# Low parts of the mixers' weights: a negated high part plus an accumulating DMA in place of a subtraction

## The chip, the cores and the metric

One Trainium2 chip, one core. The metric is the device time of one execution in microseconds (us), the median of several runs. The engines are called PE or TensorE (matrix products), DVE or VectorE, ACT or ScalarE, POOL or GpSimd, and SP or SyncE, which here issues the loads.

## The reference

A decoder trunk of two layers on 512 tokens of width 1024 in float32. Cut to what matters:

```python
def hybrid_layer(x, mem, pos, layer_idx, ...):
    proj = rms_norm(x, norm_mix) @ w_in              # one combined input projection
    if layer_idx % 2 == 0:
        mix, qm = dsa_mixer(proj, pos)               # index scores, top 128 keys of a query, softmax attention
    else:
        mix, qm = dilated_mixer(proj, pos)           # three groups of dilated windows, merged
    mo = memory_attention(qm, mem, norm_mem, w_mem_kv)   # 4 heads on 256 memory tokens
    x = x + concat([mix, mo]) @ w_out                # one combined output projection
    return x + swiglu_ffn(rms_norm(x, norm_ffn), w_gate_up, w_down)
# two layers, then a final rms_norm
```

## The kernel before

Activations lie transposed in SBUF, 128 rows of the width by 512 tokens. Every product of float32 numbers is made of three products in a format with a shorter mantissa, fp32r: a weight is split into a high part `wh` (the weight rounded) and a low part `wl` (what is left), an activation into `xh` and `xl`, and TensorE adds wh·xh, wh·xl and wl·xh (lines 200 to 202, 213 to 215, 225 to 227 and 405 to 407). For a tile of 128 columns of weights and 512 tokens these are 24 matrix products.

Weights come from DRAM by `load` (line 176 issues it on SP) into `wf`, 128x2048 float32 with two buffers; each half of 128x1024 is then split by `wsplit` into one of three buffers `wh` and one of three `wl`. `_split2` does it in two instructions: a cast, on ScalarE (line 48) or VectorE (line 50), and a subtraction `wl = wf - wh`, on VectorE or POOL (line 51). Who does which is set by arguments. There are 55 such splits of 128x1024 in the mixers:

- `chunks` gives the column tiles of an input projection or of the memory's keys, two to a load: in layer 0 tiles 2 to 14 of `in0` and 2 of `mk0`, in layer 1 2 of `mk1` and 14 of `in1`. The first tile of a load is subtracted on POOL, the second on VectorE; tiles 6 to 14 of `in0` both on POOL.
- `token_weights` gives weights with the tokens as output rows, for values (`vw0`; `mv0`, `mv1` of the memory; `v1` three times). The first half is subtracted on VectorE, the second on POOL; for `v1` the first half's cast is on VectorE too.
- `out_proj` gives the output projections (`out0a`, `out0b`, `out0c`, `out1a`, `out1b`, 12 splits): the cast on VectorE, the subtraction on POOL.

The first two weights of layer 0 and all of the feed-forward parts are split elsewhere by the same `wsplit`.

The order of TensorE's instructions is written out by hand. Those of the other engines are placed by a scheduler when the program is built; it goes by costs of its own and not by a run. An engine works through its list in that order and waits at the head of it. In layer 0 the memory's squares and their sum (`mem`, `ssq`, lines 282 and 294) are on POOL, with tables of line 373 and products of lines 338 and 339; VectorE has the top-k (lines 702 and 703: 48 maximum searches, each followed by a replacement), evictions of the memory's values (`vm`, line 387) and row maxima (`nm`, line 557). Products land in PSUM, in 2 banks of `acc`, 3 of `S`, 2 of `T` and 1 of `O`.

## Time and profile before

| | |
|---|---|
| three runs | 1286.81, 1294.6, 1292.8 us |
| median | 1292.8 us |
| profiled execution | span 1288.0 us from first to last instruction (its time with what lies around the span is not listed) |
| granted clock of TensorE | 0.974 of full speed, mean |
| TensorE busy | 1212.7 us, 94% |
| VectorE, ScalarE, POOL busy | 626.6, 532.1, 402.6 us |
| read from DRAM | 106 MB |

The table's busy times are sums over the whole span; the stages differ. Layer 0's mixer runs to about 313 us, its feed-forward part to 672, layer 1's mixer to 907 and its feed-forward part and the final norm to the end. In the rows further down, a trace line has its start in us from the span's start, its length in us, the engine, the line of the kernel, the operation, output and inputs with their shapes, and in brackets the idle time of the engine just before it and what ended that.

### The profile page before, as it was taken

What the parts mean: (1) busy time and instruction counts of PE and PEld (TensorE: products, weight loads), DVE (VectorE), ACT (ScalarE), POOL (GpSimd) and SP (SyncE); (2) the same over time, 40 slices, a digit from 0 to 9 for tenths busy, and PEclk for the clock granted to TensorE, in tenths of its full rate; (3) what the DMA queues carried; (4) which work ended last, traced back from release to release, by engine and by line L of the source; (5) the groups of instructions that cost most, each with busy time, mean ns of one, the idle gap of its engine ahead of it and who ended that gap; (6) DMA issues with size and microseconds to landing.
All of it is one profiled execution on the core that took longest, in us unless ns stands there. A gap on an engine that the chain in (4) does not pass through costs nothing.

```text
span 1288.0 us, 15199 instructions
## 1 busy us (share of the span) xinstructions
PE 1212.7 (94%) x5868; PEld 996.6 (77%) x5868; DVE 626.6 (49%) x1154; ACT 532.1 (41%) x941; POOL 402.6 (31%) x250
## 2 busy tenths in 40 slices
PE   6689888998999999999998999999999999999997
PEld 4567667776888888888886779897788888888887
DVE  7789978758433333332214554548733333331212
ACT  6554667744322233322223666644433222322222
POOL 4637475436222222212232213232522222221222
PEclk9789999999999999999998999989999999999999
DMA  5402222111222222222233110101122222222221
GB/s 179 132 32 70 80 84 96 53 63 66 95 91 90 91 93 98 98 90 102 90 110 115 66 66 34 66 34 66 66 98 98 98 98 98 98 83 97 91 90 66
DMA packets 30214, 110.52 MB, mean 86 GB/s; under 512 B 2494, under 2 KB 11582, under 8 KB 21694
## 3 DMA queue, kind: packets, MB, share of 16 engines
q1 hardware_dynamic: 29598, 109.02, 24.0%
q8 instruction: 46, 0.75, 0.2%
q10 hardware_dynamic: 544, 0.52, 0.1%
q14 instruction: 26, 0.21, 0.0%
HBM read 106.00 MB, written 3.54 MB: 85 GB/s over the span
## 4 chain that ended last, share of the span: by engine, by line
PE 74%; DVE 4%; ACT 2%; DMA 1%; issue 1%; SPq 0%; DVEq 0%; ACTq 0%
PE psS L227 5%; PE psS L226 5%; PE psS L225 4%; PE psT L227 3%; PE psT L226 3%; PE psT L225 3%; PE psacc L227 3%; PE psacc L226 3%; PE psacc L225 3%; PE psS L200 3%; PE psS L202 3%; PE psS L201 3%; PE psacc L200 3%; PE psacc L201 3%; PE psacc L202 3%; PE psacc L213 2%
## 5 line engine op out<-in xcount | busy, mean ns | idle before, releaser
L51 POOL TENSOR_TENSOR wl<-wf,wh 128x1024 fp32r<-128x1024 f32 x98 | 239.4, 2444 | 660.3 <-ACT wh L48 614.7
L48 ACT CAST wh<-wf 128x1024 fp32r<-128x1024 f32 (+1 forms) x178 | 183.5, 1032 | 515.9 <-issue 165.2
L51 DVE TENSOR_TENSOR wl<-wf,wh 128x1024 fp32r<-128x1024 f32 (+1 forms) x95 | 115.6, 1217 | 86.7 <-ACT wh L48 86.7
L225 PE MATMUL psS<-xh,wh 128*128 128x512 f32 x296 | 117.5, 397 | 7.4 <-ACT wh L48 7.4
L226 PE MATMUL psS<-xl,wh 128*128 128x512 f32 x296 | 117.2, 396 | 2.9 <-DVE xl L310 2.9
L227 PE MATMUL psS<-xh,wl 128*128 128x512 f32 x296 | 118.0, 399 | 1.1 <-DVE wl L51 0.7
L225 PE MATMUL psT<-xh,wh 128*128 128x512 f32 x200 | 80.0, 400 | 0.0
L227 PE MATMUL psT<-xh,wl 128*128 128x512 f32 x200 | 79.9, 400 | 0.0
L226 PE MATMUL psT<-xl,wh 128*128 128x512 f32 x200 | 79.7, 398 | 0.0
L227 PE MATMUL psacc<-xh,wl 128*128 128x512 f32 x192 | 76.0, 396 | 0.0
L226 PE MATMUL psacc<-xl,wh 128*128 128x512 f32 x192 | 75.7, 394 | 0.0
L225 PE MATMUL psacc<-xh,wh 128*128 128x512 f32 x192 | 75.3, 392 | 0.0
L225 PEld LDWEIGHTS psS<-xh,wh 128*128 128x128 f32 x296 | 56.2, 190 | 20.6 <-ACT wh L48 7.9
L226 PEld LDWEIGHTS psS<-xl,wh 128*128 128x128 f32 x296 | 56.3, 190 | 16.6 <-DVE xl L310 3.3
L227 PEld LDWEIGHTS psS<-xh,wl 128*128 128x128 f32 x296 | 56.3, 190 | 14.2 <-DVE wl L51 2.2
L294 POOL TENSOR_TENSOR ssq<-ssq,t 128x512 f32<-128x512 f32 (+1 forms) x34 | 49.1, 1444 | 57.7 <-ACT t L284 56.6
L659 DVE TENSOR_TENSOR raw<-psacc,R 128x512 f32<-128x512 f32 x22 | 15.2, 691 | 100.8 <-PE psacc L227 100.8
L213 PE MATMUL psacc<-xh,wh 128*128 128x512 f32 x144 | 62.7, 435 | 0.4 <-DVE vm L387 0.4
L215 PE MATMUL psacc<-xh,wl 128*128 128x512 f32 x144 | 58.4, 406 | 0.0
L214 PE MATMUL psacc<-xl,wh 128*128 128x512 f32 x144 | 58.4, 406 | 0.0
L339 POOL TENSOR_TENSOR raw<-raw,table 128x512 f32<-128x512 f32 x21 | 27.1, 1291 | 71.8 <-ACT raw L336 52.1
L634 DVE TENSOR_TENSOR xT<-xT,psacc 128x512 f32<-128x512 f32 x44 | 29.9, 684 | 34.7 <-PE psacc L202 34.3
(355 smaller groups left out, 2947.3 us busy)
## 6 DMA issues: line engine op xcount, KB each, us to landing
wf<-in_gu SPq DMA_DIRECT2D x44, 1024.0 KB
wf<-in_dn SPq DMA_DIRECT2D x16, 1024.0 KB
wf<-in_in SPq DMA_DIRECT2D x13, 1024.0 KB
wf<-in_dn SPq DMA_DIRECT2D x16, 384.0 KB
wf<-in_v SPq DMA_DIRECT2D x3, 1024.0 KB
xT<-in_x SPq DMA_DIRECT2D x8, 256.0 KB
wf<-in_mk SPq DMA_DIRECT2D x2, 1024.0 KB
wf<-in_mv SPq DMA_DIRECT2D x2, 1024.0 KB
```

Of the source, the lines that this page charges most:

```text
L48: nc.scalar.copy(hi, src)
L51: lo_engine.tensor_tensor(out=lo, in0=src, in1=hi.bitcast(F32), op=ALU.subtract)
L200: mm(out, wh[k], xh[k], start=first and k == 0, stop=False)
L201: mm(out, wh[k], xl[k], start=False, stop=False)
L202: mm(out, wl[k], xh[k], start=False, stop=last and k == n - 1)
L213: mm(out, wh[:, s], xh[k], start=k == 0, stop=False)
L214: mm(out, wh[:, s], xl[k], start=False, stop=False)
L215: mm(out, wl[:, s], xh[k], start=False, stop=k == KT - 1)
L225: mm(out, wh[:, s], xh[k], start=k == 0, stop=False)
L226: mm(out, wh[:, s], xl[k], start=False, stop=False)
L227: mm(out, wl[:, s], xh[k], start=False, stop=k == KT - 1)
L294: engine.tensor_tensor(out=parts[part], in0=parts[part], in1=sq, op=ALU.add)
```

## The change

A new function `wsplit_dma` takes the place of `wsplit` for all 55 splits. ScalarE casts the high part; ScalarE or POOL writes minus the high part into `wl` (ScalarE as the rounded weight times minus one); then a DMA issued on POOL reads the same weights again from DRAM and adds them to `wl` as it writes. The data are 0.5 MB in each, 28 MB in all. The high part, cast on VectorE in 15 places before, is now always ScalarE's.

```diff
+    def wsplit_dma(self, w, src, negate):
+        nc = self.nc
+        n = w.shape[-1]
+        wh = self.wp.tile([128, 1024], F32R, tag="wh", bufs=3, name="wh")[:, :n]
+        wl = self.wp.tile([128, 1024], F32R, tag="wl", bufs=3, name="wl")[:, :n]
+        nc.scalar.copy(wh, w)
+        if negate is nc.scalar:
+            nc.scalar.activation(wl, w, AF.Copy, scale=-1.0)
+        else:
+            negate.tensor_scalar(wl, wh.bitcast(F32), -1.0, None, op0=ALU.mult)
+        out = wl if len(src.shape) == 2 else wl.rearrange("p (t n) -> p t n", t=src.shape[1])
+        nc.gpsimd.dma_start(out=out, in_=src, accum_op=ALU.add)
+        return wh, wl
...
-    def chunks(self, name, order, lo=("gpsimd", "vector"), hi=(None, None)):
+    def chunks(self, name, order, lo=("gpsimd", "scalar")):
...
-                yield self.wsplit(w[:, j], getattr(self.nc, lo[j]), hi[j])
+                yield self.wsplit_dma(w[:, j], src[order[a] + j], getattr(self.nc, lo[j]))
...
-    def token_weights(self, src, n, deep=False):
+    def token_weights(self, src, n):
...
-            h, l = self.wsplit(w[:, c * 4 * n:(c + 1) * 4 * n], (self.nc.vector, self.nc.gpsimd)[c], (self.nc.vector, None)[c] if deep else None)
+            b = slice(c * 4 * n, (c + 1) * 4 * n)
+            h, l = self.wsplit_dma(w[:, b], src[:, b], (self.nc.scalar, self.nc.gpsimd)[c])
...
     def out_proj(self, name, outs):
-                wh, wl = self.wsplit(ww, nc.gpsimd, nc.vector)
+                wh, wl = self.wsplit_dma(ww, src[a + b:a + b + step].rearrange("t p n -> p t n"), nc.gpsimd)
```

In layer 1 the calls lose their arguments; tiles 6 to 14 of `in0` keep theirs, so their negations are all on POOL, while elsewhere in `chunks` the second tile of a load is negated on ScalarE. `mk0`, `mk1` and tiles 2 to 5 of `in0` are called as before:

```diff
...
-        ws = self.chunks("in1", list(range(14)), lo=("gpsimd", "vector"), hi=(None, None))
+        ws = self.chunks("in1", list(range(14)))
...
-            w = self.token_weights(self.io["v1"][g], 256, True)
+            w = self.token_weights(self.io["v1"][g], 256)
```

The scheduler puts the other engines' instructions in a new order. Three places of it follow. In each, line numbers are those of the file that the rows come from: in the changed file a line of the old one stands 15 or 16 lines further down (line 282 is 297, 294 is 309, 373 is 388, 387 is 402, 557 is 573, 702 and 703 are 718 and 719).

POOL in layer 0 when the memory's load arrives, before: `wl_251` and `wl_408` are tiles 2 and 4 of `in0`, `mem` the memory, `ssq_366` its sum of squares.

```order
L51 TENSOR_TENSOR wl_251<-wf_248,wh_250 128x1024
L51 TENSOR_TENSOR wl_408<-wf_405,wh_407 128x1024
L282 TENSOR_TENSOR ssq_366<-mem_278 128x256
L282 TENSOR_TENSOR t_368<-mem_278 128x256
L282 TENSOR_TENSOR t_371<-mem_280 128x256
```

In the changed kernel, POOL's rows at the same place; `wl_329` is tile 3 and `wl_410` tile 4:

```order
L189 TENSOR_SCALAR wl_251<-wh_250 128x1024
L191 DMA wl_251<-in_in0 128x1024
L191 DMA wl_329<-in_in0 128x1024
L189 TENSOR_SCALAR wl_410<-wh_409 128x1024
L297 TENSOR_TENSOR ssq_368<-mem_279 128x256
L297 TENSOR_TENSOR t_370<-mem_279 128x256
L191 DMA wl_410<-in_in0 128x1024
```

The two subtractions stood ahead of the memory's squares; now tile 4's negation stands there and its DMA behind two of the squares.

POOL at the end of the memory's sum, before: `wl_574` is the second half of `vw0`, the tables are those of the rotary positions times the norm of the tokens.

```order
L294 TENSOR_TENSOR ssq_366<-ssq_366,t_383 128x256
L282 TENSOR_TENSOR t_386<-mem_284 128x256
L294 TENSOR_TENSOR ssq_366<-ssq_366,t_386 128x256
L373 TENSOR_TENSOR table_446<-raw_447,R_293 128x512
L51 TENSOR_TENSOR wl_574<-wf_567,wh_573 128x1024
L373 TENSOR_TENSOR table_450<-raw_451,R_293 128x512
```

In the changed kernel, where `wl_574` and `wl_579` are the two halves of `vw0`:

```order
L191 DMA wl_574<-in_vw0 128x1024
L309 TENSOR_TENSOR ssq_368<-ssq_368,t_385 128x256
L297 TENSOR_TENSOR t_388<-mem_285 128x256
L388 TENSOR_TENSOR table_449<-raw_450,R_294 128x512
L388 TENSOR_TENSOR table_453<-raw_454,R_294 128x512
L189 TENSOR_SCALAR wl_579<-wh_578 128x1024
L309 TENSOR_TENSOR ssq_368<-ssq_368,t_388 128x256
```

The last addition to the sum moved from ahead of the two tables to behind them and a negation.

VectorE in the top-k, before, from the 21st replacement of 48 to the first eviction of the memory's values and the first row maxima:

```order
L703 MATCH_REPLACE score_399<-m8_1583,score_399 128x256
L51 TENSOR_TENSOR km_1035<-t_1036,km_1035 128x256
L702 MAX m8_1586<-score_401 128x8
L387 SCALAR_TENSOR_TENSOR vm_1075<-psacc_1050,rs_keep_483,vm_1075 128x2x64
L702 MAX m8_1589<-score_400 128x8
```

And in the changed kernel, the last row ahead of the eviction being the 31st replacement:

```order
L718 MAX m8_1633<-score_402 128x8
L718 MAX m8_1636<-score_401 128x8
L719 MATCH_REPLACE score_403<-m8_1630,score_403 128x512
L130 TENSOR_TENSOR strided_1139<-o_1125 128x128
L402 SCALAR_TENSOR_TENSOR vm_1088<-psacc_1063,rs_keep_487,vm_1088 128x2x64
```

The eviction moved behind ten more replacements, and the first row maxima (line 557, now 573) from behind 24 to behind 36.

In layer 1, the subtraction on POOL for the second half of the last of the three `v1` weights stood ahead of a product of line 339 (now 354). Its negation stands there now, and its DMA behind that product.

## Rows read from the trace of the kernel before

**Rows 1.** Page, part 1: busy time, share and instructions of each engine.

```profile
PE 1212.7 (94%) x5868; PEld 996.6 (77%) x5868; DVE 626.6 (49%) x1154; ACT 532.1 (41%) x941; POOL 402.6 (31%) x250
```

**Rows 2.** Waits of TensorE: total us, times, longest.

```profile
PE psacc L256 <- POOL ssq L294: 8.5, 1, 8.5
...
PE psS L416 <- DVE nx L602: 6.6, 7, 2.3
...
PE psS L416 <- DMA kept<-kept: 5.1, 1, 5.1
```

**Rows 3.** Timeline of TensorE: start, duration, operation, idle time before it.

```profile
43.90 0.39 PE L227 MATMUL psT<-xh,wl 128*128 128x512 f32 x1
...
58.99 1.02 PE L256 MATMUL psacc<-ones,ssq 128*128 128x2 f32 x4 [8.51 <-POOL ssq L294]
...
124.58 0.58 PE L407 MATMUL psacc<-wl,mh 128*128 128x256 f32 x1 [1.49 <-DVE wl L51]
...
179.09 0.79 PE L416 MATMUL psS<-k,qh 64*128 64x256 f32 x2 [2.27 <-DVE nx L602]
...
843.24 0.40 PE L407 MATMUL psacc<-wl,xh 128*128 128x256 f32 x1
```

**Rows 4.** Instructions by line and shape: busy us, mean ns, idle before.

```profile
L51 POOL TENSOR_TENSOR wl<-wf,wh 128x1024 fp32r<-128x1024 f32 x98 | 239.4, 2444 | 660.3 <-ACT wh L48 614.7 <-DVE wh L50 26.2 <-PE psacc L202 5.1
...
L48 ACT CAST wh<-wf 128x1024 fp32r<-128x1024 f32 x162 | 170.1, 1051 | 466.4 <-issue 157.4 <-PE psS L226 74.7 <-PE psS L201 46.0
...
L51 DVE TENSOR_TENSOR wl<-wf,wh 128x1024 fp32r<-128x1024 f32 x79 | 100.3, 1270 | 86.7 <-ACT wh L48 86.7
...
L50 DVE CAST wh<-wf 128x1024 fp32r<-128x1024 f32 x15 | 12.7, 849 | 10.4 <-PE psacc L406 3.9 <-PE psacc L201 3.8 <-PE psacc L214 2.5
...
L437 POOL COPY raw<-den 128x512 f32<-128x512 f32 x10 | 6.8, 688 | 9.3 <-DVE den L460 9.3
```

**Rows 5.** Windows: busy us of PE, PEld, DVE, ACT, POOL; clock, DMA share.

```profile
64.00:96.00 32.00, 26.33 (x158) 20.98 (x157) 26.01 (x46) 18.25 (x42) 10.47 (x8) 0.84 0.09 33
128.00:160.00 32.00, 28.52 (x173) 22.30 (x173) 32.00 (x83) 20.66 (x54) 13.62 (x11) 0.95 0.23 83
192.00:224.00 32.00, 27.04 (x195) 22.62 (x195) 26.79 (x69) 26.59 (x70) 15.81 (x11) 1.00 0.31 111
```

**Rows 6.** Timelines of SP's queue and of ScalarE around one load.

```profile
116.29 0.34 SPq L176 DMA_DIRECT2D wf<-in_mv  x1
...
121.21 1.99 ACT L48 CAST wh<-wf 128x1024 fp32r<-128x1024 f32 x2 [1.91 <-DMA wf<-in_mv]
```

**Rows 7.** Chain that ended last, 670 to 720 us: start, duration, what.

```profile
691.19 12.93 DMA kept<-kept
```

**Rows 8.** Timeline of POOL, 20 to 68 us.

```profile
20.78 4.22 POOL L51 TENSOR_TENSOR wl<-wf,wh 128x1024 fp32r<-128x1024 f32 x1 [5.63 <-ACT wh L48]
29.17 2.40 POOL L51 TENSOR_TENSOR wl<-wf,wh 128x1024 fp32r<-128x1024 f32 x1 [4.17 <-ACT wh L48]
43.04 0.62 POOL L282 TENSOR_TENSOR ssq<-mem 128x256 f32<-128x256 f32 x1 [11.47 <-DMA mem<-in_mem]
...
57.89 1.05 POOL L294 TENSOR_TENSOR ssq<-ssq,t 128x256 f32<-128x256 f32 x1
...
63.37 1.30 POOL L373 TENSOR_TENSOR table<-raw,R 128x512 f32<-128x512 f32 x1 [0.42 <-DMA raw<-saved]
```

**Rows 9.** Line 703 on VectorE: ns min/median/max, first and last start.

```profile
L703 DVE MATCH_REPLACE8 score<-m,score x48: 399/542/681, 105.5 to 174.7; 128x512 f32<-128x512 f32 x16, 128x384 f32<-128x384 f32 x16, 128x256 f32<-128x256 f32 x16
```

**Rows 10.** Timeline of VectorE, 130 to 135 us.

```profile
130.36 0.33 DVE L387 SCALAR_TENSOR_TENSOR vm<-psacc,rs_keep,vm 128x128 fp32r<-128x128 f32 x1
...
133.84 1.28 DVE L557 TENSOR_REDUCE nm<-psS 128x2 f32<-128x512 f32 x2
```

**Rows 11.** Timeline of POOL in layer 1, 835 to 841 us.

```profile
835.70 2.41 POOL L51 TENSOR_TENSOR wl<-wf,wh 128x1024 fp32r<-128x1024 f32 x1 [0.96 <-ACT wh L48]
839.10 1.29 POOL L339 TENSOR_TENSOR raw<-raw,table 128x512 f32<-128x512 f32 x1 [0.99 <-ACT raw L336]
```

## Prediction

> **What bounds the kernel now.** I read the page's line of busy times first: TensorE works 1212.7 us, 94% of the span [rows 1]. No change to the other engines can give back more than the 75 us that are left, and any lateness of theirs counts only where TensorE then stands still. So the next view is what TensorE waited for [rows 2]: the longest single wait, 8.5 us, is for the memory's sum of squares on POOL, then come evictions of VectorE and one reload of 5.1 us. Low parts of weights hardly appear there: the longest wait for one that I found in TensorE's timeline is 1.49 us, before 124.58 [rows 3]. Subtractions on POOL and VectorE are therefore long work (239.4 and 100.3 us for whole tiles [rows 4]) but hidden work. The table by stretches says where there is no room: from 128 to 160 us VectorE is busy for all of its 32 us, and from 192 to 224 us ScalarE for 26.59 of 32 [rows 5].
>
> **The price of one new low part.** Before: the cast (1.05 us), then a subtraction of 2.44 us on POOL or 1.27 us on VectorE [rows 4]. After: the cast, a negation, an issue on POOL, and the transfer's landing. On ScalarE a negation is a copy of 128x1024 like the cast, 1.05 us. On POOL no such operation is in the trace; half its size, a copy with one input of 128x512, takes 0.69 us [rows 4], so 1.4 us, and at most the 2.44 us of the subtraction. POOL issues no such DMA before: the nearest row, an issue by SP, takes 0.34 us [rows 6], the other end is a whole subtraction (2.4 us); I take 1 us, between the two and nearer SP's. Landing: a load of 1 MB issued at 116.29 was there when ScalarE cast it at 121.21, 4.9 us [rows 6]. An accumulating transfer of 0.5 MB has to read 0.5 MB of DRAM and 0.5 MB of SBUF, so I estimate about the same, 5 us. Bounds: somewhat over 3 us if only the half megabyte counts, and 12.9 us, which a reload took while the queue was full of others [rows 7]. Together 7.4 us from cast to use where it was 1.3 to 2.4: 5 to 6 us later for each of 55 splits. In work: VectorE loses 18 subtractions and 15 casts (0.85 us [rows 4]), 36 us; ScalarE gains as many negations and casts, 35 us; POOL makes 37 negations for 37 subtractions and issues 55 transfers, 107 us for 90. None of the three is full over the span, so these sums matter only in the two full stretches.
>
> The Trainium skill has a fit for just this path in "DMA: Bandwidth & Descriptors", section "Anatomy of one DMA — SWDGE (gpsimd) path": about 2 us plus the bytes over 436 kB per us. That would be 3.2 us for 512 KB (an estimate), less than the 4.9 us that the row shows for twice the bytes; by it the two terms of layer 1 below would shrink by some 1.8 us each, and the sum would be about 15 us instead of 19. No run shown here has an accumulating transfer.
>
> Most of these 5 to 6 us are covered. There are three buffers of each kind, and the split of the fifth tile was ready at 31.57 (29.17 and 2.40) [rows 8] for a use at 43.90 [rows 3], 12.3 us ahead. What can't be covered is where the distance is shorter than that, and where the order of an engine moves. I go by stages.
>
> **Start and the memory's norm (0 to 104 us).** In POOL's new order the DMA for wl_410 (tile 4) stands behind two squares of the memory. The first of those began in the old run at 43.04, after 11.47 us of waiting for the memory's load [rows 8]. With two of 0.62 us and an issue of 1 us it is under way at 45.3 and lands near 50.3, where TensorE wants it at 43.90 [rows 3]: a stall of some 6.4 us that was not there. It doesn't add up with what follows: TensorE anyway stood 8.51 us before the sum of squares at 58.99 [rows 3]. That sum moves. Its last addition on POOL, from 57.89 to 58.94 [rows 8], was made before the two tables; now it stands behind both tables and a negation. The second table began at 63.37 and took 1.30, waiting for its own load [rows 8]; with the negation (1.4) and the addition (1.05) the sum ends at 67.1 instead of 58.94, and three DMA issues on POOL before it cost their microsecond each only as far as the wait for the table doesn't swallow them. So TensorE goes on 8 us later. Between 64 and 96 us it idles 5.7 of 32 us [rows 5], and VectorE and ScalarE have used the time to run ahead, so some of it comes back; I take back 4, and add 2 because the memory's own load now shares the DMA engines with half a megabyte of accumulation: **+6** (bounds +2, all idle time recovered; +10, none and a slow landing).
>
> **Top-k (104 to 180 us).** VectorE makes the top-k's 48 replacements from 105.5 to 174.7, with a maximum search before each [rows 9]; it is without a gap for most of that [rows 5], so the order of its queue is what counts. Before, the first value of the memory (vm) came behind 21 replacements, at 130.36, and the first row maxima (nm) behind 24, at 133.84 [rows 10]. In the new order vm stands behind 31 and nm behind 36. A replacement takes 0.54 us at the median [rows 9], its maximum search about as much, so a pair costs 1.1 us: 10 pairs are 11 us, 12 pairs 13 us; one subtraction of 1.27 us leaves the queue. TensorE waits for these evictions since it has two accumulation banks and three banks for scores. It has 3.5 idle us from 128 to 160 [rows 5] to take some of that up, and the end of the top-k itself (TensorE goes on at 179.09 behind a maximum on VectorE [rows 3]) moves by the work in front of it: **+8** (bounds +5, +11). The low parts of the memory's value weights were used as soon as they were there (124.58 [rows 3]); 5 us later on this path is inside the 8, since VectorE's delay ends last. If that transfer took 10 us, it would add 6.
>
> **Rest of layer 0's mixer (180 to 313 us).** VectorE loses two subtractions and eight casts of 0.85 us [rows 4], ScalarE gains the casts at 1.05 us and two negations while it is the busy engine [rows 5]. Gain and loss meet: **0** (−3, +4).
>
> **Both feed-forward parts** use the old function: 0.
>
> **Layer 1's mixer (672 to 907 us).** The second half of the third group's value weights was ready at 838.11 (835.70 and 2.41) [rows 11] for a use at 843.24 [rows 3], 5.1 us ahead. On POOL its DMA now stands behind the multiplication that ran from 839.10 to 840.39 [rows 11]; issued by 841.4, landed at 846.4: +3. The wait of 5.1 us for the reload [rows 2] sits in a stretch in which its transfer took 12.93 us in a full queue [rows 7]; another megabyte of accumulation in it is worth +2. No other low part of that stage is among the waits [rows 2] or as tight in POOL's new order: **+5** (0, +9).
>
> Sum: 6 + 8 + 0 + 5 = **+19 us** on a span of 1288.0, with bounds of +4 and +34. The profiled span lies 4.8 us below the median of the three runs and above the fastest of them, 1286.81, so I put what lies around it at nothing that changes and add the sum to the median: 1292.8 + 19 = **1311 us**, to the nearest.
>
> **The rivals.** *Hidden altogether*: the order of the queues only shows what waits, and if landing takes 3 us, the memory's norm and the top-k absorb their shifts in idle time that TensorE has there anyway (8.5 us before the sum alone). For it: 94% of TensorE is busy and hardly a low part was waited for. Against it: VectorE has no gap in the top-k. Then −6 to +8, about 1294 us.
>
> *Slow accumulation*: each transfer takes 10 to 13 us as the crowded reload did [rows 7], not 5. Then the chain is 13 to 15 us, longer than the 5.1 and 12.3 us ahead of the two splits above, and if some ten more are like them and each adds 3 to 4 us, that is +30 to +60, about 1330 us. For it: small runs of 1 to 2 KB in the output projections; against it: the plain load of 4.9 us.
>
> *Faster, because VectorE and POOL are freed*: the price is paid in two-input subtractions. One on POOL took 4.22 us at 20.78 instead of 2.40 [rows 8], so engines hinder each other; with 55 of them gone VectorE gets back some 36 us of its own, of which those in the full stretch from 104 to 180 us count. If four or five us there and the 2 to 3 us of the late start are won, and DMA lands in time, the time is −6 to −20, about 1281 us. It decides when vm and nm come on time although they stand later in the queue. "SBUF — State Buffer", section "Who interferes with whom", in the Trainium skill says that a VectorE instruction with two inputs in SBUF contends with a POOL instruction that reads SBUF; the 4.22 us agrees with that, but no other row separates the cause.
>
> That the change doesn't do what it says I hold for impossible: the new order contains the DMAs.
>
> **How the numbers follow.** Forecast (+8 to +30) 0.52; hidden 0.24; slow 0.14; faster 0.10. Repeats of this kernel lie 0.6% apart, so about 1% is what a measurement can tell: 1279.9 and 1305.7. Faster by over 1%: two thirds of the last rival and a little of the hidden one, 0.08. Slower: four fifths of the forecast (0.42) and all of the slow rival (0.14), 0.56. Same: the rest, 0.36. The range leaves out 0.1 on either side: from 1288 (the lower part of the hidden case in it) to 1336 (half of the slow case).
>
> **What would show it.** In the changed profile: POOL's DMA issues take about 1 us and land 5 us on (over 10: the slow rival); TensorE stands still before the low part of tile 4 near 44 to 51 us, and before the sum of squares until 67; vm and nm come near 141 and 146 us; the end of the top-k stands by the same time later in the span; TensorE waits for a low part near 846. If TensorE's idle time from 0 to 180 us has not grown by 10 us or more, the forecast's main terms are wrong. What I know least is the landing of the accumulation.

## The result and the profile after

The changed kernel takes 1327.3 us (median of 4 runs, 1326.4 to 1336.3) where the kernel before takes 1292.9: 1.0284 times as long, 95% interval 1.0238 to 1.0331, some 34 us. The forecast was 1311 us, slower, with a range to 1336: the direction was right and the time lies in the range, but the loss is twice the 18 us forecast. The span is 1325.3 us, 37.3 us longer than [rows 1]'s. One execution of the first experiment below took 2357 us and is left out of its median.

The page's line of busy times and two rows of its list of DMA queues (packets, MB, share of the time of 16 engines):

```profile
PE 1217.2 (92%) x5868; PEld 1001.6 (76%) x5868; DVE 579.5 (44%) x1122; ACT 562.6 (42%) x973; POOL 461.1 (35%) x305
...
q1 hardware_dynamic: 29598, 109.02, 23.7%
q0 software_dynamic: 11504, 28.84, 13.0%
```

TensorE works 1217.2 us, 4.5 us more than before. Its idle time went from 75.3 us (1288.0 − 1212.7) to 108.1 us (1325.3 − 1217.2), so 32.8 of the 37.3 us are waiting; the other 4.5 are matmuls that ran longer, under a mean granted clock of 0.962 where it was 0.974. VectorE works 47 us less than before and that buys nothing. Queue q0 is new: its 28.84 MB keep the DMA engines busy for 13.0% of the span, where the 109 MB of q1's plain loads need 23.7%: per MB twice as long.

The waits of TensorE (total us, times, longest), which answer to [rows 2]:

```profile
PE psT L242 <- DMA wl<-in_in: 10.6, 1, 10.6
PE psacc L271 <- POOL ssq L309: 10.0, 1, 10.0
PE psacc L423 <- DMA wl<-in_mv: 9.3, 2, 5.1
PE psS L242 <- DMA wl<-in_in: 7.7, 1, 7.7
PE psS L432 <- DMA kept<-kept: 7.4, 1, 7.4
...
PE psacc L423 <- DMA wl<-in_v: 5.8, 2, 3.8
...
PE psacc L230 <- DMA wl<-in_mk: 2.2, 1, 2.2
```

Before, the longest wait for a low part was 1.49 us [rows 3]. Now the added transfers are waited for 35.6 us in these rows (10.6 + 9.3 + 7.7 + 5.8 + 2.2; the 7.7 are for tile 2, the 10.6 for tile 4), and the reload of 5.1 us became 7.4.

TensorE's timeline at the matmuls of [rows 3], and at one more in between (154.81, the second low part of the memory's values):

```profile
57.69 0.79 PE L242 MATMUL psT<-xh,wl 128*128 128x512 f32 x1 [10.59 <-DMA wl<-in_in]
...
77.00 0.80 PE L271 MATMUL psacc<-ones,ssq 128*128 128x2 f32 x3 [10.00 <-POOL ssq L309]
...
146.81 0.58 PE L423 MATMUL psacc<-wl,mh 128*128 128x256 f32 x1 [4.23 <-DMA wl<-in_mv]
...
154.81 0.58 PE L423 MATMUL psacc<-wl,mh 128*128 128x256 f32 x1 [5.08 <-DMA wl<-in_mv]
...
206.26 0.59 PE L432 MATMUL psS<-k,qh 64*128 64x256 f32 x2 [0.58 <-DVE nx L618]
...
880.64 0.60 PE L423 MATMUL psacc<-wl,xh 128*128 128x256 f32 x1 [3.76 <-DMA wl<-in_v]
```

Read against [rows 3] these give the lateness as it grows: 13.8 us at tile 4's low part (43.90 then), 18.0 at the memory's sum (58.99), 22.2 at the first low part of the memory's values (124.58), 27.2 after the top-k (179.09), 37.4 at the last value weights (843.24). One such pair of rows for each stage says more than the two spans: the loss is made in the first 160 us and, a sixth of it, in layer 1.

POOL's timeline of the start, which answers to [rows 8]:

```profile
20.89 4.68 POOL L189 TENSOR_SCALAR wl<-wh 128x1024 fp32r<-128x1024 f32 x1 [5.64 <-ACT wh L185]
...
28.14 0.86 POOL L191 DMA_DIRECT2D wl<-in_in  x1 [1.18 <-ACT wl L187]
28.85 2.97 POOL L189 TENSOR_SCALAR wl<-wh 128x1024 fp32r<-128x1024 f32 x1
48.24 0.61 POOL L297 TENSOR_TENSOR ssq<-mem 128x256 f32<-128x256 f32 x1 [16.42 <-DMA mem<-in_mem]
48.82 1.05 POOL L297 TENSOR_TENSOR t<-mem 128x256 f32<-128x256 f32 x1
49.82 0.89 POOL L191 DMA_DIRECT2D wl<-in_in  x1
...
72.25 1.26 POOL L388 TENSOR_TENSOR table<-raw,R 128x512 f32<-128x512 f32 x1 [7.71 <-DMA raw<-saved]
73.49 2.77 POOL L189 TENSOR_SCALAR wl<-wh 128x1024 fp32r<-128x1024 f32 x1
76.24 0.71 POOL L309 TENSOR_TENSOR ssq<-ssq,t 128x256 f32<-128x256 f32 x1
```

Negations take 2.8 us and more. The memory's first square waits 16.42 us for its load and starts at 48.24, 5.2 us later than before; two squares stand ahead of the issue at 49.82, whose transfer TensorE gets at 57.69. The second table waits for its reload until 72.25 (63.37 before), and behind it stand a negation and the last addition, which ends at 76.95.

Why the memory came late can be seen on SP, which issues its load in four parts, before and after:

```profile
31.13 5.69 SPq L469 DMA_DIRECT2D mem<-in_mem  x4
```

```profile
31.22 10.73 SPq L485 DMA_DIRECT2D mem<-in_mem  x4
```

The four issues begin at the same time but take 10.73 us instead of 5.69, so the last one is out 5.1 us later. That is nearly all of the 5.2 us by which the memory's first square is late: the delay arises while SP issues, not after it.

All negations on POOL in one row (count, ns min/median/max). Of the transfers, the 27 issues for `in0` and `in1`, and the landings of all 55, which this view counts from the start of the issue:

```profile
L189 POOL TENSOR_SCALAR wl<-wh x38: 2762/2772/4685, 20.9 to 916.3; 128x1024 fp32r<-128x1024 f32 x38
```

```profile
L191 POOL DMA_DIRECT2D wl<-in_in x27: 850/891/1357, 25.9 to 857.9; - x27
...
DMA to landing us min/median/max: 5.1/6.1/10.0
```

The chain that ended last has the reload of [rows 7] at 15.62 us instead of 12.93:

```profile
721.88 15.62 DMA kept<-kept
```

Last, two rows around the memory's values, of ScalarE and of VectorE, to be read with [rows 10]:

```profile
157.35 0.37 ACT L401 ACTIVATE vm<-psacc,rs_keep 128x128 fp32r<-128x128 f32 x1 [13.42 <-PE psacc L423]
```

```profile
157.75 0.35 DVE L402 SCALAR_TENSOR_TENSOR vm<-psacc,rs_keep,vm 128x128 fp32r<-128x128 f32 x1 [1.63 <-ACT vm L401]
```

ScalarE waited 13.42 us for TensorE's product, and VectorE for ScalarE. So VectorE did not come last, but it was close: its queue had reached this eviction at 156.12 us (157.75 − 1.63), 25.8 us later than in [rows 10].

### The profile page after: what moved, and what is told of

The parts are those of the page before. It is cut to its first block, busy times and chain, and to the rows that moved or that the text cites. A ratio compares the mean times of both kernels' runs of the same rounds, so it can differ in the third digit from the quotient of the medians.

```text
span 1325.3 us, 15297 instructions
## 1 busy us (share of the span) xinstructions
PE 1217.2 (92%) x5868; PEld 1001.6 (76%) x5868; DVE 579.5 (44%) x1122; ACT 562.6 (42%) x973; POOL 461.1 (35%) x305
## 3 DMA queue, kind: packets, MB, share of 16 engines
q1 hardware_dynamic: 29598, 109.02, 23.7%
q0 software_dynamic: 11504, 28.84, 13.0%
## 4 chain that ended last, share of the span: by engine, by line
PE 67%; DVE 3%; ACT 3%; DMA 2%; issue 1%; DVEq 0%; POOL 0%; ACTq 0%
PE psS L241 5%; PE psS L242 4%; PE psS L240 4%; PE psT L241 3%; PE psT L240 3%; PE psT L242 3%; PE psacc L241 3%; PE psacc L240 3%; PE psacc L242 3%; PE psS L215 3%; PE psS L217 3%; PE psS L216 3%; PE psacc L215 2%; PE psacc L217 2%; PE psacc L216 2%; PE psO L241 1%
## 5 line engine op out<-in xcount | busy, mean ns | idle before, releaser
L48 ACT CAST wh<-wf 128x1024 fp32r<-128x1024 f32 (+1 forms) x138 | 141.9, 1029 | 472.5 <-issue 163.8
L51 POOL TENSOR_TENSOR wl<-wf,wh 128x1024 fp32r<-128x1024 f32 x60 | 145.3, 2421 | 516.9 <-ACT wh L48 516.9
L189 POOL TENSOR_SCALAR wl<-wh 128x1024 fp32r<-128x1024 f32 x38 | 109.3, 2876 | 106.4 <-ACT wh L185 88.0
L242 PE MATMUL psS<-xh,wl 128*128 128x512 f32 x296 | 118.1, 399 | 10.2 <-DMA wl<-in_in 7.7
L51 DVE TENSOR_TENSOR wl<-wf,wh 128x1024 fp32r<-128x1024 f32 x78 | 94.7, 1214 | 68.2 <-ACT wh L48 68.2
L242 PE MATMUL psT<-xh,wl 128*128 128x512 f32 x200 | 80.1, 401 | 10.6 <-DMA wl<-in_in 10.6
L185 ACT CAST wh<-wf 128x1024 fp32r<-128x1024 f32 x55 | 57.7, 1049 | 58.4 <-PE psacc L216 16.2
```

The costliest lines, as they stand in the source:

```text
L48: nc.scalar.copy(hi, src)
L51: lo_engine.tensor_tensor(out=lo, in0=src, in1=hi.bitcast(F32), op=ALU.subtract)
L185: nc.scalar.copy(wh, w)
L189: negate.tensor_scalar(wl, wh.bitcast(F32), -1.0, None, op0=ALU.mult)
L242: mm(out, wl[:, s], xh[k], start=False, stop=k == KT - 1)
```

## The experiments

For each run there is the ratio to the kernel before, timed on the same chip. Since several parts of the loss interact, I also read each profile as above: how late the same matmul is against [rows 3] and, below, how much longer each mixer is in all. The mixers are measured on TensorE's timeline, layer 0's from the start of the span to the matmul at 276.02 us of the old span, layer 1's from the one at 678.57 to the one at 937.11. All of this is worked out as differences of two starts, from one profile of each kernel.

| kernel | ratio, 95% interval | late at 58.99 | at 124.58 | at 179.09 | mixer 0 longer | mixer 1 longer |
|---|---|---|---|---|---|---|
| the change | 1.0284 (1.0238 to 1.0331) | 18.0 | 22.2 | 27.2 | 30.3 | 6.2 |
| start by subtraction | 1.0232 (1.0178 to 1.0287) | −0.4 | 6.7 | 12.2 | 21.1 | 7.8 |
| memory by subtraction | 1.0230 (1.0185 to 1.0274) | 18.4 | 15.5 | 16.9 | 26.9 | 6.6 |
| plain transfers | 1.0172 (1.0122 to 1.0223) | 13.2 | 12.6 | 18.8 | 25.6 | 0.1 |
| last addition on VectorE | 1.0296 (1.0250 to 1.0343) | 6.4 | 16.9 | 21.8 | 30.5 | 7.9 |
| only layer 1 changed | 1.0128 (1.0084 to 1.0172) | 0.6 | 2.7 | 2.7 | 3.5 | 9.2 |
| only output projections | 1.0028 (0.9999 to 1.0057) | 0.3 | 1.1 | 1.1 | 4.6 | 1.2 |
| no transfers | 0.9980 (0.9957 to 1.0003) | −2.4 | −7.3 | −10.1 | −1.1 | −0.6 |
| only splits far ahead | 1.0157 (1.0125 to 1.0188) | 0.1 | 0.2 | 1.8 | 11.4 | 4.3 |
| tiles 2, 3 by subtraction | 1.0256 (1.0213 to 1.0299) | 3.3 | 14.7 | 19.8 | 29.3 | 8.9 |
| tiles 4, 5, vw0 by subtraction | 1.0211 (1.0159 to 1.0263) | 6.7 | 13.1 | 19.7 | 22.8 | 8.1 |
| an eighth of the bytes | 1.0151 (1.0108 to 1.0194) | 10.2 | 6.3 | 17.0 | 21.9 | 2.3 |
| negations on VectorE | 1.0135 (1.0081 to 1.0188) | 3.5 | 4.1 | 11.6 | 18.1 | 2.7 |
| the same, plain transfers | 1.0091 (1.0059 to 1.0124) | 0.8 | −3.1 | 4.4 | 10.7 | −0.8 |
| far ahead, negations on VectorE | 1.0038 (1.0004 to 1.0071) | 0.1 | −2.4 | 1.3 | 9.0 | −3.5 |

The mixers don't make up the whole difference. TensorE, at full granted clock and never idle, goes through a feed-forward part at two rates. These windows from 460 to 520 us are of the changed kernel and of the first experiment (stretch; busy us and count of PE, PEld, DVE, ACT, POOL; granted clock, DMA share, GB/s).

```profile
460.00:520.00 60.00, 60.00 (x264) 49.23 (x263) 22.19 (x29) 17.98 (x22) 12.07 (x5) 1.00 0.28 102
```

```profile
460.00:520.00 60.00, 60.00 (x259) 48.61 (x258) 19.08 (x25) 16.57 (x21) 14.26 (x6) 1.00 0.25 91
```

264 and 259 matmuls in 60 us, both at clock 1.00. At the slower rate a feed-forward part is 4 to 6 us longer. Which rate a profile shows does not go with the transfers: in the profile of the change both parts have the faster rate, in that without any transfer both have the slower one (4.1 and 4.7 us longer). Medians of few runs carry that, so differences under some 6 us are read from the mixers. These too have a spread: in the five runs that leave layer 1 as in the change (the first two, the last addition, and the two on tiles 2 to 5) mixer 1 is 6.6 to 8.9 us longer, where the change has 6.2. Less than 3 us in a mixer says nothing.

A second thing stands between a wait and the time: the granted clock. These windows hold the same 554 matmuls, from the one at 179.09 to the one at 276.02 us of the old span, in the kernel before, the change, memory by subtraction, only splits far ahead, and the last row of the table.

```profile
179.09:276.02 96.93, 87.51 (x554) 70.44 (x555) 67.81 (x190) 70.45 (x190) 44.12 (x32) 0.98 0.20 66
```

```profile
206.26:306.32 100.06, 88.96 (x554) 71.64 (x555) 61.00 (x183) 76.82 (x197) 59.55 (x44) 0.97 0.48 112
```

```profile
195.98:302.96 106.98, 91.87 (x554) 73.85 (x555) 58.55 (x183) 77.12 (x197) 58.84 (x44) 0.92 0.45 104
```

```profile
180.85:287.47 106.62, 91.54 (x554) 73.55 (x555) 58.55 (x183) 77.12 (x197) 58.89 (x44) 0.92 0.46 105
```

```profile
180.36:285.01 104.65, 93.00 (x555) 75.27 (x555) 65.76 (x190) 77.15 (x197) 37.62 (x34) 0.92 0.46 106
```

TensorE is idle there (the stretch less its busy time) for 9.4, 11.1, 15.1, 15.1 and 11.7 us and busy for 87.5, 89.0, 91.9, 91.5 and 93.0 us; the longer work goes with the lower mean granted clock (1.00 is the upper of its two levels, 2.4 GHz). So part of what a run wins before 179 us is lost after it in slower matmuls, not in waits.

**Start by subtraction.** Tiles 2 to 5 of `in0` and `vw0` are split as before (`old=True` calls the old `wsplit`).

```diff
-        ws = itertools.chain(self.chunks("in0", [2, 3]), self.chunks("in0", [4, 5]),
+        ws = itertools.chain(self.chunks("in0", [2, 3], lo=("gpsimd", "vector"), old=True), self.chunks("in0", [4, 5], lo=("gpsimd", "vector"), old=True),
...
-            w = self.token_weights(self.io["vw0"], 256)
+            w = self.token_weights(self.io["vw0"], 256, old=True)
```

> The changed kernel, but tiles 2 to 5 of in0 and both halves of vw0 are split by subtraction as before. In the changed kernel TensorE is 18 us late when the memory's sum of squares arrives and still 17 to 18 us late at 104 us of the old span. Theory: the six accumulating transfers of the start cause all of it, by their own landings and by holding up reloads in a busy queue, so about 17 us go: 1310 us. Rival: the lateness of the start is made up later anyway (VectorE's top-k or ScalarE would be late next), then 5 us or less go: 1322 us or more.

Measured: 1324.9 us, ratio 1.0232, the time that the rival forecast. All 18 us at the memory's sum are gone, but mixer 0 is only 9 us shorter, and the other half comes back between 59 and 276 us. So the rival holds for half: a late start hides losses that come later. What is left at the memory's values (6.7 at 124.58, 12.2 at 179.09) is that stage's own loss.

**Memory by subtraction.** `mk0` and `mv0` as before.

```diff
-        for w in self.chunks(f"mk{l}", [0, 1]):
+        for w in self.chunks(f"mk{l}", [0, 1], lo=("gpsimd", "scalar" if l else "vector"), old=l == 0):
...
-        w = self.token_weights(self.io[f"mv{l}"], 256)
+        w = self.token_weights(self.io[f"mv{l}"], 256, old=l == 0)
```

> The changed kernel, but the memory's keys and values of layer 0 (mk0, mv0) are split by subtraction as before. Theory: between 104 and 155 us TensorE loses 9.5 us only by waiting for these four low parts, so 8 to 10 us go: 1318 us, and the evictions of the memory's values come as soon as the products are there. Rival, the one of the prediction: the place of the evictions behind more rounds of the top-k in VectorE's order ends last, then TensorE waits for VectorE there and only 0 to 4 us go, if the order stays as in the changed kernel, and the gain comes only with an order like the old one.

Measured: 1326.9 us, ratio 1.0230. From 18.4 us late at the sum, TensorE is 16.9 late at 179.09, where the change is 27.2 late: 10 us go in that stage, as the theory said. Seven of them come back by 276 us, 4 as idle time and 3 as longer work under the lower clock (windows above): mixer 0 is 3.4 us shorter, and the whole time is not the 1318 us of the theory. VectorE's order is another one here, so the run alone doesn't refute the prediction's reason; the two rows of ScalarE and VectorE above show only that in the change the low parts came last, by 1.6 us.

**Plain transfers.** Same order on every engine, without the accumulation.

```diff
-        nc.gpsimd.dma_start(out=out, in_=src, accum_op=ALU.add)
+        nc.gpsimd.dma_start(out=out, in_=src)
```

> The changed kernel with every added transfer as a plain copy of the same bytes that does not add: the addition is left out, so wl holds the weight itself; order and waits stay. In the changed kernel a packet of 4 KB of an accumulating transfer keeps a DMA engine for 350 ns, one of a plain load 170 ns. Theory: the accumulation doubles the engine time and so delays itself and the reloads beside it; plain, the landing falls from 6.1 us to about 4, the memory's load lands 2 to 4 us earlier, and 8 to 15 us of the 34 go: 1313 to 1320 us. Rival: negation and issue on POOL and the place in the order cost the time, whatever the transfer does: within 4 us of the changed kernel.

Measured: 1317.6 us, ratio 1.0172: 10 us of medians and 1.1% of ratios, as the theory said. The landings and the new queue's row:

```profile
DMA to landing us min/median/max: 3.7/4.3/8.0
```

```profile
q0 software_dynamic: 11504, 28.84, 7.6%
```

4.3 us in place of 6.1, and 7.6% of the engines' time in place of 13.0%. Mixer 1 is 0.1 us longer instead of 6.2, though TensorE still waits there 1.8 us for a low part and 6.0 for the reload; 5 us of the start go. But a plain transfer still costs 1.7%.

**Last addition on VectorE.** Only the addition that ended at 76.95 us moves.

```diff
-        for m in mem:
-            add(m, 0, self.nc.gpsimd, self.nc.gpsimd)
+        for k, m in enumerate(mem):
+            add(m, 0, self.nc.vector if k == KT - 1 else self.nc.gpsimd, self.nc.gpsimd)
```

> The changed kernel with only the last addition of the memory's sum of squares on VectorE instead of POOL; the order of POOL stays, and so this addition no longer waits behind two tables and a negation. Theory A (place in the order): TensorE gets the sum near 66 instead of 77 us, and some of the 11 us are lost again to the second low part of vw0, which lands near 86: 4 to 9 us go, 1318 to 1323 us. Theory B (only landings of reloads count, and the second table, which arrives at 72 us, holds up TensorE next anyway): within 3 us of the changed kernel.

Measured: 1335.9 us, ratio 1.0296, no gain: in the whole time theory B's forecast is the nearer one. TensorE's rows:

```profile
65.39 0.39 PE L271 MATMUL psacc<-ones,ssq 128*128 128x2 f32 x3
...
84.54 0.58 PE L423 MATMUL psT<-wl,xh 128*128 128x256 f32 x1 [7.76 <-DMA wl<-in_vw]
```

The sum comes at 65.39, 11.6 us earlier and within 1 us of what theory A said. Then the second low part of `vw0` is waited for 7.76 us, and of 11.6 us 5.3 are left at 124.58. At 276 us none is left. So the place in the order decides which wait comes first here, and another one stands behind it.

**Only layer 1 changed.** All of layer 0 by subtraction: the edits of the first two runs, and

```diff
+                if name in ('out0a', 'out0b', 'out0c'):
+                    wh, wl = self.wsplit(ww, nc.gpsimd, nc.vector)
...
-                             self.chunks("in0", list(range(6, 15)), lo=("gpsimd", "gpsimd")))
+                             self.chunks("in0", list(range(6, 15)), lo=("gpsimd", "gpsimd"), old=True))
```

> Only layer 1's 28 splits and those of its memory (mk1, mv1, in1, v1, out1a, out1b) by the new way, all of layer 0 by subtraction as before. In the changed kernel layer 1's mixer is 6.2 us longer than before. Theory: that part doesn't depend on layer 0, so layer 0's mixer takes the old time and layer 1's 6 us more: 1296 to 1301 us where the kernel before has 1293. Rival: what layer 1 loses hangs on the lateness that layer 0 brings, then 1293.

Measured: 1307.4 us, ratio 1.0128. Mixer 1 is 9.2 us longer, mixer 0 3.5 (layer 1's memory is split there), and one feed-forward part ran at the slow rate. The theory holds in kind, with 9 in place of 6, though its 1296 to 1301 us were too few; layer 1's loss needs no late layer 0.

**Only output projections.** The 12 splits of `out_proj` by the new way, all others by subtraction: layer 0's edits as above but for that of `out_proj`, both layers' memory, and

```diff
-        ws = self.chunks("in1", list(range(14)))
+        ws = self.chunks("in1", list(range(14)), lo=("gpsimd", "vector"), old=True)
...
-            w = self.token_weights(self.io["v1"][g], 256)
+            w = self.token_weights(self.io["v1"][g], 256, old=True)
```

> Only the 12 splits of the output projections by the new way (cast on ScalarE, negation and transfer on POOL), all others by subtraction. Their low parts were ready 9 to 32 us ahead of their use, the way is 7 us longer. Theory (landing against distance ahead): no low part is waited for, within 3 us of the kernel before. Rival (engines relieved): VectorE, which loses 12 casts and sat in the chain before some of them, makes it 4 us faster or more. Rival (ScalarE loaded): 4 us slower or more in the stretch from 180 to 313 us.

Measured: 1294.9 us, ratio 1.0028 (0.9999 to 1.0057): no difference that counts. Neither a gain from VectorE's lost casts nor much of a loss.

**No transfers.** All negations and casts as in the change, the transfers left out.

```diff
-        nc.gpsimd.dma_start(out=out, in_=src, accum_op=ALU.add)
```

> The changed kernel with the negations and without any of the 55 added transfers: the addition is left out, wl is minus the high part. The scheduler puts the engines in another order for it. Theory: the transfers, not the negations or the casts on ScalarE, cost the time, so the time comes back to the kernel before, 1288 to 1297 us, and TensorE's waits for the tables and the memory in the first 80 us are as before. Rival: a negation on POOL of 2.8 us, no shorter than a subtraction, and casts moved to ScalarE cost a third or more: 1304 us or more.

Measured: 1289.7 us, ratio 0.9980 (0.9957 to 1.0003). The whole loss goes with the transfers, though the 38 negations on POOL take 2.86 us each, as they did (2.88). With them goes the order that the scheduler makes for them: at the memory's sum POOL's list is the old one again. The run is also the price of all that the change could win: with VectorE relieved and no landing to wait for it is 0.2%, which the interval doesn't tell from nothing. That is the price in this order of the engines: TensorE is 10.1 us early at 179.09 and has lost nine of them again at 276.02, with a clock of 0.92 between.

**Only splits far ahead.** Tiles 6 to 14 of `in0`, `mk1`, `mv1` and the output projections by the new way; the edits are those of the first two runs and of the one with only output projections.

> The new way only where low parts are ready far ahead: tiles 6 to 14 of in0, mk1 and mv1, all output projections, 25 of 55 splits; by subtraction tiles 2 to 5 of in0, vw0, mk0, mv0, in1 and v1. Theory (landing against distance ahead): within 5 us of the kernel before, no wait of TensorE for an added transfer. Rival (any added transfer costs, by the traffic in the queues and on POOL): 25 of 55 of 34 us, about 1308 us.

Measured: 1312.1 us, ratio 1.0157. The theory fell: no transfer is among TensorE's longer waits, and still 11.4 us go in mixer 0. By the windows above 5.7 us of them are idle time after 179.09 and 4.0 longer work. A row of POOL's timeline in that stage, one of VectorE's, and the wait of TensorE that hangs on them:

```profile
198.27 1.26 POOL L357 TENSOR_TENSOR raw<-raw,table 128x512 f32<-128x512 f32 x1 [4.14 <-ACT raw L354]
```

```profile
200.79 0.29 DVE L624 CUSTOM_DVE_ANT_0 raw<-psS,window 128x128 f32<-128x128 f32 x1 [4.44 <-POOL ql L51]
```

```profile
PE psS L438 <- DVE nx L624: 11.3, 9, 4.4
```

VectorE waits 4.44 us for POOL's low part of a query (line 51), which follows this rotary product; and POOL had itself just waited 4.14 us for ScalarE's copies. So the last link here is ScalarE. Whether POOL's negations and issues, which stand further ahead in its list (180.94 to 192.83), made ScalarE late, the rows don't say; the last experiment tests it.

**Tiles 2 and 3 by subtraction**, and the reverse, **tiles 4, 5 and vw0 by subtraction**: the parts of the first run's edit.

> The changed kernel with only tiles 2 and 3 of in0 by subtraction; tiles 4 and 5 and vw0 keep their transfers. Of the 18 us that the start loses, the theory (transfers hold up the reloads) puts half on these two: their 1 MB runs from 28 to 38 us in the queue of the tables' and the memory's reloads. So the memory lands near 43 to 44 us, not 48, the wait before tile 2's low part is gone, and TensorE gets the memory's sum 7 to 11 us earlier than in the changed kernel, near 66 to 70 us. Rival (place in POOL's order): the sum still comes at 74 to 77 us, since the transfers of tiles 4, 5 and vw0 and the tables stand before it as they did. Of the whole time I expect only part, as single undone parts gave 7 us or less so far: 1318 to 1327 us.

> The reverse: tiles 4 and 5 of in0 and vw0 by subtraction, tiles 2 and 3 by transfer. Theory (held up reloads): the memory still lands near 48 us and TensorE waits 7 us for tile 2's low part; the sum comes at 65 to 69 us, because the second table, whose reload is free of vw0's transfer, comes earlier and stands no longer before it. Rival (place in POOL's order): the sum comes near 59 to 62 us, as before. Whole time 1318 to 1327 us.

Measured: 1328.4 us (1.0256) and 1324.7 us (1.0211). POOL's first square of the memory in the one and in the other:

```profile
43.79 0.61 POOL L300 TENSOR_TENSOR ssq<-mem 128x256 f32<-128x256 f32 x1 [10.96 <-DMA mem<-in_mem]
```

```profile
48.03 0.65 POOL L300 TENSOR_TENSOR ssq<-mem 128x256 f32<-128x256 f32 x1 [16.63 <-DMA mem<-in_mem]
```

Without the two transfers the memory's load is there within 0.8 us of the old time (43.04 in [rows 8]); with them alone it is there at 48.03. SP's four issues take 5.80 us in the one and 10.38 in the other. So these two transfers beside the load are what made it late. The sum was at 62.32 and 65.65: the first earlier than I expected, since the addition also got ahead of the second table in that order. In the first run TensorE then waits 7.8 us for the second low part of `vw0`.

**An eighth of the bytes.** Every transfer still accumulates, on 128 of 1024 columns.

```diff
-        nc.gpsimd.dma_start(out=out, in_=src, accum_op=ALU.add)
+        nc.gpsimd.dma_start(out=out[..., :out.shape[-1] // 8], in_=src[..., :out.shape[-1] // 8], accum_op=ALU.add)
```

> The changed kernel with every added transfer cut to the first eighth of its columns, still accumulating: the addition for the rest of the columns is left out. Number, issue and waits of the transfers stay. Theory (bytes: landing and the engine time of the accumulation): a landing of 2.5 to 3.5 us in place of 6.1, TensorE loses under 5 us in the start and under 4 at the memory's values; 1296 to 1306 us. Rival (the number of transfers, their issues on POOL and their waits): 1313 us or more.

Measured: 1315.4 us, ratio 1.0151. My theory fell again: the landing is as short as it said,

```profile
DMA to landing us min/median/max: 2.6/3.0/6.3
```

and yet half of the loss stays. (The order of the engines differs from the change's in some places.) Bytes and accumulation are one half; the other hangs on each transfer's presence, with its negation and its issue. The second low part of `mv0` is still waited for 6.5 us, and behind it stands a wait that the prediction had named, for an eviction of the memory's values on VectorE:

```profile
148.99 0.47 PE L228 MATMUL psacc<-xh,wh 128*128 128x512 f32 x1 [3.20 <-DVE vm L402]
```

**Negations on VectorE.** POOL keeps the 55 issues, its 38 negations go to VectorE.

```diff
-            negate.tensor_scalar(wl, wh.bitcast(F32), -1.0, None, op0=ALU.mult)
+            nc.vector.tensor_scalar(wl, wh.bitcast(F32), -1.0, None, op0=ALU.mult)
```

> The changed kernel with the 37 negations of POOL on VectorE; POOL keeps the issues of all transfers, and the one of tile 4 now stands ahead of the memory's squares. Theory (transfers: landing, and reloads held up): the memory still lands near 48 us and the memory's values and v1 still wait for their transfers; what the place on POOL cost in the start goes (the wait for tile 4's low part, the sum behind the tables), some 8 us at 60 us of which later waits take half: 1318 to 1325 us. Rival (POOL's list, with 2.8 us for each negation ahead of the issues, is what makes low parts late): 1308 us or less.

Measured: 1312.4 us, ratio 1.0135, between the two: 15 us of the medians go. A negation there takes 0.75 us (mean of 38):

```profile
L189 DVE TENSOR_SCALAR wl<-wh 128x1024 fp32r<-128x1024 f32 x38 | 28.5, 750 | 19.4 <-ACT wh L185 19.2
```

**The same with plain transfers**, the two edits together.

> The changed kernel with POOL's negations on VectorE and with plain transfers that do not add (the addition is left out); same order as with VectorE's negations alone, which took 1312 us. Theory: place on POOL (15 us so far) and the accumulation's slow packets (10 us alone) are separate costs that add up, so 9 to 13 us more go: 1300 to 1304 us, and a remainder of 8 to 11 us is the landing of a plain transfer, 4 us and more. Rival: the two costs are one, a chain that is too long somewhere and shortened by either, then 1308 us or more.

Measured: 1305.8 us, ratio 1.0091. In ratios, POOL's list alone gave back 1.5%, the accumulation alone 1.1%, both together 1.9% of 2.8%. Taken as they stand these are two costs with about a quarter of their sum in common, but the intervals are some half a percent to either side, as wide as that quarter. The mixers say more plainly that the second edit adds to the first: both together are 20.8 us longer with the negations on VectorE alone, and 9.9 with both edits. 0.9% is left for the issues, a plain landing and what hangs on them.

**Only splits far ahead, negations on VectorE.**

> The kernel with the new way only where low parts are ready far ahead (tiles 6 to 14 of in0, mk1, mv1, all output projections), which took 1312 us, with POOL's negations on VectorE. Theory: there the loss is not a late low part but POOL's list, with negations and issues ahead of rotary products (VectorE waited 4.4 us for one of them); then most of it goes, 1296 to 1302 us. Rival: the traffic of the 25 transfers or VectorE's and ScalarE's new order costs it, then 1308 us or more.

Measured: 1297.2 us, ratio 1.0038 (1.0004 to 1.0071), where POOL's negations gave 1.0157. The wait from above:

```profile
PE psS L438 <- DVE nx L624: 5.3, 7, 2.1
```

The whole time is what the theory said, and TensorE's idle time from 179.09 to 276.02 falls from 15.1 to 11.7 us, near the old 9.4. So POOL's negations made more than half of the added waiting there, and not the transfers. But mixer 0 is still 9.0 us longer, where it was 11.4, 5.5 of it by longer work at a clock of 0.92; and of the 15 us between the medians some may be the feed-forward parts, which both ran slow in the profile with POOL's negations and both fast in this one. So the rival of the traffic and the other engines' order is not ruled out for what is left. With only output projections (1.0028) this is the best form of the new way here, and neither is faster than subtraction.

## Why the prediction was half right

**The bound and the kind of loss** were right. TensorE's idle time is where it was lost, at the places named: tile 4's low part, the memory's sum, the memory's values, the last `v1` weights and the reload in layer 1. Both feed-forward parts took nothing beyond their two rates. Two readings were slightly off, and nothing in the sum hangs on them: POOL makes 38 negations and ScalarE 17, not 37 and 18; and among TensorE's waits in the kernel before, 7.4 us for ScalarE's casts come ahead of those for VectorE.

**The step that failed is the sum for the start**, +6 us (bounds +2 and +10), which measured 18.0 at the memory's sum and 17.8 at the stage's end (105.59 us of the old span became 123.40). The path was the forecast one: the last addition to the sum waits behind two tables and a negation. It was to end at 67.1 us and ended at 76.95. Of these 9.8 us 8.9 are the second table, whose own reload the forecast left at its old time (63.37; it came at 72.25), and 1.4 the negation, taken as 1.4 us from a copy of half its size, with 2.44 us as its upper bound: it took 2.77, with one input where the subtraction has two. With plain transfers, and the same order, that table comes at 67.46. So the term that was put at nothing is that the added transfers hold up the table's reload; for the memory's load it was put at 2 us and was 5.2 (48.24 against 43.04), shown by the two runs on tiles 2 to 5. A wait for tile 2's low part (7.7 us) was not forecast, but like the one for tile 4 it lies ahead of the sum and doesn't add to it. And the 4 us that were to be taken back in TensorE's idle time were not taken back: 18.0 us at the sum are 17.8 at the stage's end.

**The price of a transfer** was right: the issue takes 0.89 us where I took 1, and from its start to the landing it is 6.1 us where I took 6 (1 and 5). What an accumulating transfer moves the profile doesn't show; it keeps the DMA engines busy 1.7 times as long as a plain one on the same queue. The Trainium skill's fit in "DMA: Bandwidth & Descriptors", section "Anatomy of one DMA — SWDGE (gpsimd) path", gives 3.2 us for 512 KB (an estimate). From the start of the issue the runs show 4.3 us for a plain transfer and 6.1 for an accumulating one, so here the measurement decides.

**Top-k**: +8 forecast, 9.4 measured (27.2 − 17.8), but for another reason. Not the evictions' place behind more rounds on VectorE, but the low parts of `mv0`, 9.3 us of waiting, and of `mk0`, 2.2. On POOL the issue for the second half of `mv0` stood 3.7 us behind its negation, with a split of queries and another negation between (143.04 to 146.77). I had set these waits inside VectorE's delay; it was the reverse, but by 1.6 us only. VectorE's queue reached the eviction 25.8 us late, of which the start had made 17.8, so I estimate that the new order alone would have cost the 8 us forecast. Two delays of about the same length lay side by side; that the number came out near is in part luck.

**Rest of mixer 0**: 0 forecast, 3.1 measured (30.3 − 27.2), within its bounds. **Layer 1**: +5 forecast, 6.2 measured; the last `v1` weights cost 3.8 us (forecast 3), the reload 2.3 more (forecast 2), other `v1` weights 2.0 that I had not named, and with plain transfers mixer 1 is as long as before.

**The rivals.** Hidden altogether: fell. Slow accumulation at 10 to 13 us: fell, the landing's maximum is 10.0 and its median 6.1, though a loss of its size came about by way of POOL and the held-up reloads. Faster through relief: the run without transfers shows that there was next to nothing to win, since VectorE's subtractions were hidden where they stood. The one long subtraction on POOL (4.22 us) on which that rival leaned has a successor as long: the negation at 20.89 takes 4.68 us, and no run separates why.

What stays open: the start, the memory and the rest don't add up, since undoing one lets another wait come forward, in part through the scheduler's new order, and since the granted clock is lower in some of these runs (0.92 and not 0.97 in the windows above). I can't say how much of each is the order, the clock or the landing; no run has the change's own order and no transfers. Nor do the runs show why TensorE has two rates at full clock.

## What to carry to other kernels

Work that is hidden has no price, so taking it off an engine wins nothing; look first at what a run without the replacement would win, here 0.2%. A transfer in place of an instruction turned 1.3 to 2.4 us of latency into 7 to 9 here (a negation of 1.05 us on ScalarE or 2.77 on POOL, then 6.1 from issue to landing), and it must be ahead of its use by that, in the list of the engine that issues it too: everything that stands ahead of the issue there counts. And added traffic is paid by the loads that are issued beside it, on another queue too, and not only by its own user.

## What was unexpected

- A negation of 128x1024 with one input takes POOL 2.77 us, longer than its subtraction with two (2.44), and VectorE 0.75 us.
- Two accumulating transfers of 0.5 MB on POOL's queue stretched SP's four issues of the memory's load from 5.69 to 10.73 us.
- An accumulating transfer keeps the DMA engines busy 1.7 times as long as a plain one of the same bytes on the same queue (13.0% against 7.6% of the span), and lands in 6.1 us in place of 4.3; one of 64 KB still takes 3.0 us.
- TensorE at full granted clock and without idle time made 264 matmuls in 60 us in one profile and 259 in another.
